# Low parts of weight tiles made by an accumulating DMA instead of DVE subtractions, in a two-layer diffusion block

## The chip, the core and the metric

The kernel runs on one core of one Trainium2 chip. The metric is the device time of one execution in microseconds (us), given as the median of several runs. The engines are called as the profile calls them: PE (matrix multiplications; PEld is its loading of weights), DVE (vector engine), ACT (scalar engine), POOL (GpSimd) and SP (the engine that here only issues loads). The profile also shows the clock that PE was granted, as a share of full speed.

## What is computed

The reference is a block with two layers on 512 latent tokens `x` and 256 context tokens, of width 1024, all in float32. Cut to what matters:

```python
for l in range(2):
    mod = (silu(c) @ w_mod[l] + b_mod[l])            # shifts, scales, gates; the same for c_ctx
    px = (rmsnorm(x, norm1_g[l]) * (1 + sc1) + sh1) @ w_in[l] + b_in[l]
    pc = (rmsnorm(xc, norm1_g[l]) * (1 + scc1) + shc1) @ w_in[l] + b_in[l]
    # columns of px, pc: four mLSTM heads in both directions | spatial gating | convolution
    x = x + g1 * (mix(px) @ w_out[l])
    x = x + g2 * swiglu(rmsnorm(x, norm2_g[l]) * (1 + sc2) + sh2, w_gu[l], w_down[l])
    if l == 0:                                       # the same two lines for the context xc
        ...
return rmsnorm(x, final_g)
```

`w_gu` is 1024 x 5632 and `w_down` 2816 x 1024. Nearly all the work is the multiplication of tokens by these weights, which have to be read from memory: the kernel moves 173 MB.

## The kernel before

**Tiles.** The 768 tokens lie transposed in on-chip memory, features on the 128 partitions. A matmul takes 128 x 128 of a weight tile against 512 latent tokens (`HA`) or 256 context tokens (`HB`). Float32 accuracy comes from splitting both factors into a high part, rounded to the type that PE multiplies in (fp32r), and a low part, the remainder. Each product is then three matmuls, high by high (L453), high by low (L454) and low by high (L455), in `mm` of `tiles`. So only the third needs a weight tile's low part.

**How a weight tile is made.** SP loads it (`loader`, L327) into one of 4 `raw` buffers. ACT rounds it into `hi` (`splitter`, L412); then DVE writes `lo` = raw - hi (`split_lo`, L333), after which the raw buffer is free for another load and the tile may be used. There are 5 pairs of `hi` and `lo`; PE frees one with the last matmul of the tile. The file has 170 such plain tiles: 116 with 1024 columns a partition (512 KB), and 54 narrower ones of 544 to 896.

**Tiles of other kinds.** The weights of the modulation (`w_mod`) are multiplied in float32 as they come, without a split; those of layer 0 come first, in 16 loads of 512 KB into 10 larger buffers called `slot`, and each is used by 8 small matmuls (L595). In the FFN of layer 1, after two plain pairs of columns, 20 "pairs" of columns go through sums and differences of half tiles, as in Strassen's scheme, to save matmuls. Their high parts are cast by ACT (L350), their low parts (L354) and sums (L359) made by DVE, from two loads each (L316), and PE uses them in L1783 to L1785, whose results ACT copies out (L1851). In between stand the plain tiles of `w_down`, called d tiles here: four groups of 8, with 768, 768, 640 and 640 columns, of which three groups stand among the pairs and one at the end.

**The order of the work.** Every engine runs its instructions in the order of the program. That order is made when the program is built, by a planner (`Plan`): each piece of work is a generator that yields costs for an engine (`DVE2`, `ACT`, `POOL`, `PE`, `DMA`, from small formulas in ns), events to wait for and buffers to take, and the planner walks through time and lets the earliest go first. So a cost in these formulas doesn't change how long an instruction takes on the chip, but it does change where it and others stand in the order. For a load the planner adds 2000 ns until its data are there (`DMA_LAT`). The order of the first loads is a string, `EARLY_LOADS`.

**POOL** has little to do before: 42 small instructions for the inverse roots of the norms (L262, tiles `rs`, `srs`, `crs`, `hrs`) and some fills. It issues no DMA. At the start the first tokens are normed with such roots into `HA` and `HB`.

Of the kernel before, what the change touches and what calls it, by code (L numbers as in the profile page):

```python
# [7 lines left out]
F32 = mybir.dt.float32  # L8
F32R = mybir.dt.float32r
AF = mybir.ActivationFunctionType  # L10
ALU = mybir.AluOpType
# [46 lines left out]
class Plan:  # L58
# [12 lines left out]
    def spawn(self, gen, prio=1):  # L71
        t = self.cur.t + LAT if self.cur else 0.0
        self.start(Thread(gen, prio, t))
# [43 lines left out]
    def release(self, name, n=1):  # L117
        t = self.cur.t + LAT
        self.buf[name] += [t] * n
        self.wake(name)  # L120
# [12 lines left out]
    def fire(self, ev, extra=0.0):  # L133
        ev.t = self.cur.t + LAT + extra
        for th in ev.waiting:
            th.t = max(th.t, ev.t)
            th.engine = None
            self.start(th)
        ev.waiting = []
# [27 lines left out]
def W(ev):  # L167
    return ("w", ev)


def A(name, n=1):
    return ("a", name, n)
# [14 lines left out]
def DVE2(n):  # L187
    return ("e", "dve", 65 + 1.04 * n)
# [14 lines left out]
def ACT(n, table=None):  # L203
    return ("e", "act", 95 + 0.833 * n, table)
# [7 lines left out]
    return ("e", "dma", 20 + nbytes / 360.0)  # L212


DMA_LAT = 2000.0
EARLY_LOADS = "xxxxmmwmmww"
AHEAD = (3, 2, 3, 3)
BUFFERS = {"ps": 8, "slot": 10, "raw": 4, "spl": 5, "hp": 0, "u4": 0, "pb": 4, "wi": 3, "cp": 1, "kk": 2, "hc": 2, "C0": 5, "C1": 5}
# [3 lines left out]
def backbone(ctx, tc, xT_d, cT_d, wmod_d, wb_d, wgv_d, wv_d, wout_d, wgu_d, wd_d, sw_d, sb_d, cv_d, rv_d, id_d, mk_d, out_d):  # L222
    nc = tc.nc
    pe, dve, act, pool, sp = nc.tensor, nc.vector, nc.scalar, nc.gpsimd, nc.sync
    S = Plan(BUFFERS)
# [11 lines left out]
    def buf(tag, shape, name, dt=F32):  # L237
        return bufp.tile(shape, dt, tag=tag, name=name, bufs=BUFFERS["spl" if tag in ("hi", "lo") else tag])
# [32 lines left out]
    def ev(*key):  # L271
        if key not in EV:
            EV[key] = Event()
        return EV[key]

    def wsrc(key):
        kind = key[0]
        if kind == "b":
            return wb_d[key[1], key[2]], KD, P
        if kind == "gv":  # L280
            k0, n = GV_SLABS[key[2]]
            return wgv_d[key[1], :, k0 * 272:(k0 + n) * 272], n, 272
        if kind == "v":
            return wv_d[key[1], :, key[2] * 1024:(key[2] + 1) * 1024], 2, 512
        if kind == "o":
            return wout_d[key[1], key[2]], KD, P
        if kind == "gu":
            return wgu_d[key[1], key[2]], KD, P
        if kind == "d":
            j0, n = FFN_GROUPS[key[1]][key[2]]  # L290
            return wd_d[key[1], key[3], :, j0 * P:(j0 + n) * P], n, P
        if kind == "mod":
            return wmod_d[key[1], key[2], key[3]].rearrange("p (a b) -> p a b", a=4), 4, 256
        if kind == "modq":
            _, l, v, q, k = key
            return wmod_d[l, v, 4 * k:4 * k + 4, :, q * 256:(q + 1) * 256].rearrange("k p c -> p k c"), 4, 256
        if kind == "modh":
            _, l, v, half, k = key
            return wmod_d[l, v, 2 * k:2 * k + 2, :, half * 512:(half + 1) * 512].rearrange("k p c -> p k c"), 2, 512
        raise ValueError(kind)  # L300

    def loader():
        for i, key in enumerate(ORDER):
            if key[0] == "x":
                yield DMA(P * T * 8)
                sp.dma_start(out=xT[:, key[1]:key[1] + 2, :], in_=xT_d[:, key[1]:key[1] + 2, :])
                fire(ev("x", key[1]), DMA_LAT)
                continue
            if key[0] == "gp":
                if key[3] == 0:  # L310
# [7 lines left out]
                    RAW[key[:3]] = rs  # L318
                    fire(ev("raw", key[:3]), DMA_LAT)
                continue  # L320
# [6 lines left out]
            sp.dma_start(out=r if key[0][:3] == "mod" else r.rearrange("p a b -> p (a b)"), in_=src)  # L327
            fire(ev("raw", i), DMA_LAT)

    def split_lo(i, hi, lo):  # L330
        r = RAW.pop(i)
        yield DVE2(r.shape[1] * r.shape[2])
        dve.tensor_tensor(lo, r, hi.bitcast(F32), ALU.subtract)  # L333
        release("raw")
        fire(ev("w", i))

# [41 lines left out]
    def split_pair(i, key):  # L378
        u, us = key[3], USET.setdefault(key[:3], {})
        if u == 3:  # L380
            return
        yield A("spl")
        us[u] = take_spl(i)
        if u:
            fire(ev("u", key[:3], u))
            return
        yield A("u4")
        us[3] = SPL[INDEX[key[:3] + (3,)]] = U4.pop(0)
        yield W(ev("raw", key[:3]))
        spawn(pair_sums(key, us), 0)  # L390
# [3 lines left out]
    def splitter():  # L394
        for i, key in enumerate(ORDER):
            if key[0] == "x":
                continue
            if key[0] == "gp":
                yield from split_pair(i, key)
                continue  # L400
            yield W(ev("raw", i))
            if key[0][:3] == "mod":
                SPL[i] = RAW.pop(i)
                fire(ev("w", i))
                continue
            _, a, b = wsrc(key)
            yield A("spl")
            hi = buf("hi", [P, a, b], "hi", F32R)
            lo = buf("lo", [P, a, b], "lo", F32R)
            SPL[i] = (hi, lo)  # L410
            yield ACT(a * b)
            act.copy(hi, RAW[i])  # L412
            spawn(split_lo(i, hi, lo), 0)

    prog = []
# [426 lines left out]
    def layer(l):  # L842
# [13 lines left out]
        def E(*key):  # L856
            return ev(l, *key)
# [47 lines left out]
        def gv_pre():  # L905
# [12 lines left out]
            for half in range(2):  # L918
                yield DMA(64 * 256 * 4)
                sp.dma_start(out=st["bs"][64 * half:64 * half + 64], in_=sb_d[l, half].partition_broadcast(64))  # L920
            fire(E("gvc"), DMA_LAT)

# [37 lines left out]
        def gates(gi):  # L960
# [87 lines left out]
            st["dr"] = dr  # L1048
            fire(E("dr"), DMA_LAT)
            yield A("ps")  # L1050
# [181 lines left out]
        def v_pre():  # L1232
# [5 lines left out]
            for i in range(2):  # L1238
                v_[i] = slot([P, 3, H, P + 1], "v")
                yield POOL(12)  # L1240
                pool.memset(v_[i][:, :, :, P:P + 1], 1.0)
            fire(E("bv"), DMA_LAT)

# [761 lines left out]
    ppos, mpos, nx = [], [], 0  # L2005
    for c in EARLY_LOADS + "m" * len(pkeys) + "w" * len(mkeys):
        n = len(ORDER)
# [17 lines left out]
    with tc.manual_schedule():  # L2025
        S.spawn(start(), 0)
        S.spawn(loader(), 3)
        S.spawn(splitter(), 0)
        S.spawn(main(), 5)
        try:  # L2030
            S.run()
        except AssertionError:
            for k, e in EV.items():
                if e.t is None and e.waiting:
                    print("EV", k, [(t.gen.__name__, t.gen.gi_frame.f_lineno) for t in e.waiting])
            raise
# [64 lines left out]
```

## Time and profile before

| What | Before |
|---|---|
| median of 3 runs | 1569.12 us (1568.55 to 1570.35) |
| profiled execution | 1569.28 us |
| its span, first to last instruction | 1567.5 us |
| mean granted clock of PE | 0.994 |
| data moved | 173.21 MB, mean 111 GB/s |

The rows of the profile that the prediction uses are shown there. A row of a group gives line, engine, operation, tiles out<-in, shapes and count, then busy us and mean ns of one, then the idle time of the engine just before these instructions and what ended it. "PE mm L453 <- ACT HA L1523: 1.2, 1, 1.2" in the list of waits says that PE, at L453, was idle for what ACT's L1523 made: us in all, how often, longest. A row of the timeline starts with the time in the span and the duration, and may end with a wait in brackets.

### The profile page before, as it was taken

What the parts mean: (1) busy time and instruction counts of PE and PEld (TensorE: products, weight loads), DVE (VectorE), ACT (ScalarE), POOL (GpSimd) and SP (SyncE); (2) the same over time, 40 slices, a digit from 0 to 9 for tenths busy, and PEclk for the clock granted to TensorE, in tenths of its full rate; (3) what the DMA queues carried; (4) which work ended last, traced back from release to release, by engine and by line L of the source; (5) the groups of instructions that cost most, each with busy time, mean ns of one, the idle gap of its engine ahead of it and who ended that gap; (6) DMA issues with size and microseconds to landing.
All of it is one profiled execution on the core that took longest, in us unless ns stands there. A gap on an engine that the chain in (4) does not pass through costs nothing.

```text
span 1567.5 us, 25687 instructions
## 1 busy us (share of the span) xinstructions
PE 1525.9 (97%) x10472; PEld 1360.0 (87%) x10472; DVE 966.2 (62%) x1934; ACT 590.3 (38%) x1128; POOL 30.9 (2%) x50
## 2 busy tenths in 40 slices
PE   4999999999999999999999999999999799999997
PEld 3887888888888888888888888878999799999997
DVE  4449877456655555433444345496777886776775
ACT  4332267543322211221122234415664454443443
POOL 0000011000000000000000000000000000000000
PEclk9999999999999999999999999999999899999999
DMA  9434344312243334433343211322331133233331
GB/s 325 150 111 140 106 131 149 141 54 82 81 136 121 110 105 136 134 120 101 130 148 109 93 62 62 102 76 88 115 109 55 55 121 95 96 101 102 105 111 55
DMA packets 69362, 173.21 MB, mean 111 GB/s; under 512 B 7180, under 2 KB 18556, under 8 KB 69244
## 3 DMA queue, kind: packets, MB, share of 16 engines
q1 hardware_dynamic: 66476, 170.16, 33.1%
q8 instruction: 82, 1.34, 0.3%
q10 hardware_dynamic: 2768, 1.42, 0.3%
q14 instruction: 36, 0.29, 0.1%
HBM read 169.34 MB, written 2.21 MB: 109 GB/s over the span
## 4 chain that ended last, share of the span: by engine, by line
PE 94%; DVE 3%; DMA 1%; ACT 1%; issue 1%; SPq 0%; POOLq 0%; POOL 0%; DVEq 0%; ACTq 0%
PE mm L453 23%; PE mm L454 22%; PE mm L455 22%; PE bA L1785 2%; PE bA L1783 2%; PE bA L1784 2%; PE vp L1224 2%; PE vp L1226 1%; PE vp L1225 1%; PE bC L1785 1%; PE bC L1783 1%; PE bC L1784 1%; PE stp L1361 1%; PE num L1445 1%; PE num L1448 1%; PE modps L575 1%
## 5 line engine op out<-in xcount | busy, mean ns | idle before, releaser
L453 PE MATMUL mm<-HA,hi 128*128 128x512 f32 (+1 forms) x928 | 347.0, 374 | 1.7 <-ACT HA L1523 1.2
L454 PE MATMUL mm<-HA,hi 128*128 128x512 f32 (+1 forms) x928 | 337.9, 364 | 1.3 <-DVE HA L790 1.0
L455 PE MATMUL mm<-HA,lo 128*128 128x512 f32 (+1 forms) x928 | 337.4, 364 | 0.0
L412 ACT CAST hi<-raw 128x1024 fp32r<-128x1024 f32 (+5 forms) x170 | 165.9, 979 | 406.4 <-PE mm L454 148.3
L333 DVE TENSOR_TENSOR lo<-raw,hi 128x1024 fp32r<-128x1024 f32 (+5 forms) x170 | 192.5, 1135 | 159.9 <-ACT hi L412 151.9
L453 PEld LDWEIGHTS mm<-HA,hi 128*128 128x128 f32 x928 | 175.1, 189 | 31.4 <-issue 4.7
L455 PEld LDWEIGHTS mm<-HA,lo 128*128 128x128 f32 x928 | 174.5, 188 | 29.9
L454 PEld LDWEIGHTS mm<-HA,hi 128*128 128x128 f32 x928 | 175.0, 189 | 25.8 <-DVE HA L790 1.9
L453 PE MATMUL mm<-HB,hi 128*128 128x256 f32 x592 | 170.1, 287 | 0.0
L823 DVE SCALAR_TENSOR_TENSOR xT<-mm,modc,xT 128x256 f32<-128x256 f32 (+1 forms) x144 | 77.4, 542 | 146.3 <-PE mm L455 145.5
L454 PE MATMUL mm<-HB,hi 128*128 128x256 f32 x592 | 165.0, 279 | 0.8 <-DVE HB L790 0.8
L455 PE MATMUL mm<-HB,lo 128*128 128x256 f32 x592 | 164.8, 278 | 0.0
L453 PE MATMUL mm<-hid,hi 128*128 128x256 f32 (+1 forms) x352 | 119.6, 340 | 0.0
L453 PEld LDWEIGHTS mm<-HB,hi 128*128 128x128 f32 x592 | 111.3, 188 | 8.8 <-issue 5.4
L455 PE MATMUL mm<-hid,lo 128*128 128x256 f32 (+1 forms) x352 | 118.7, 337 | 0.0
L454 PE MATMUL mm<-hid,hi 128*128 128x256 f32 (+1 forms) x352 | 118.4, 336 | 0.0
L454 PEld LDWEIGHTS mm<-HB,hi 128*128 128x128 f32 x592 | 112.2, 190 | 3.8 <-DVE HB L790 1.0
L455 PEld LDWEIGHTS mm<-HB,lo 128*128 128x128 f32 x592 | 111.3, 188 | 0.0
L647 DVE SCALAR_TENSOR_TENSOR macc<-raw,csil,macc 128x512 f32<-128x512 f32 x140 | 101.6, 746 | 0.7
L454 PE MATMUL mm<-ffn,hi 128*128 128x256 f32 x352 | 99.1, 282 | 0.3 <-DVE ffn L1886 0.3
L453 PE MATMUL mm<-ffn,hi 128*128 128x256 f32 x352 | 99.1, 281 | 0.1
L455 PE MATMUL mm<-ffn,lo 128*128 128x256 f32 x352 | 98.4, 280 | 0.0
(302 smaller groups left out, 2993.7 us busy)
## 6 DMA issues: line engine op xcount, KB each, us to landing
raw<-in_wmod SPq DMA_DIRECT2D x96, 512.0 KB, 3.7
raw<-in_wgu SPq DMA_DIRECT2D x88, 512.0 KB, 3.5
raw<-in_wb SPq DMA_DIRECT2D x36, 512.0 KB, 3.5
pbt<-dr SPq DMA_DIRECT2D x40, 256.0 KB, 3.6
raw<-in_wout SPq DMA_DIRECT2D x16, 512.0 KB, 3.5
raw<-in_wd SPq DMA_DIRECT2D x16, 448.0 KB, 3.9
raw<-in_wd SPq DMA_DIRECT2D x16, 384.0 KB, 3.3
raw<-in_wd SPq DMA_DIRECT2D x16, 320.0 KB, 3.0
```

The costliest lines, as they stand in the source:

```text
L333: dve.tensor_tensor(lo, r, hi.bitcast(F32), ALU.subtract)
L412: act.copy(hi, RAW[i])
L453: pe.matmul(o, lhsT=hi[:, k, :], rhs=hh, start=(j == 0), stop=False)
L454: pe.matmul(o, lhsT=hi[:, k, :], rhs=hl, start=False, stop=False)
L455: pe.matmul(o, lhsT=lo[:, k, :], rhs=hh, start=False, stop=(j == nk - 1))
L575: pe.matmul(p[32 * c:32 * c + 32, 0:256], lhsT=csil[:, k, :], rhs=s[:, c, :], start=(k == 0), stop=(k == KD - 1), skip_group_check=True)
L647: dve.scalar_tensor_tensor(a[:, g, :], s[:, i, :], c, a[:, g, :], ALU.mult, ALU.add)
L823: dve.scalar_tensor_tensor(x, p[:, 0:n], MODC[l][:, v, d, g:g + 1], x, ALU.mult, ALU.add)
L1224: pe.matmul(out, lhsT=hh, rhs=hi[:, kk, :], start=(k == 0), stop=False)
L1783: pe.matmul(o, lhsT=hi[:, k], rhs=rh[:, k], start=start and k == 0, stop=False, skip_group_check=True)
L1784: pe.matmul(o, lhsT=hi[:, k], rhs=rl[:, k], start=False, stop=False, skip_group_check=True)
L1785: pe.matmul(o, lhsT=lo[:, k], rhs=rh[:, k], start=False, stop=k == 3, skip_group_check=True)
```

## The change

`lo` is no longer a subtraction on DVE. ACT writes minus `hi` into `lo` right behind the cast (a second ACT instruction of the same size, on the same tile), and POOL then issues a DMA that adds the raw tile to it in place, element by element, so that `lo` = -hi + raw. The DMA's landing, not an instruction's end, now frees the raw buffer and makes the tile ready. The planner counts 1.0 us of POOL for the issue and 4.0 us more until it has landed. POOL's buffer for DMA descriptors is doubled. This holds for the 170 plain tiles; the pairs of layer 1's FFN keep DVE for their low parts.

```diff
+def POOLQ():
+    return ("e", "pool", 1000.0)
+
 DMA_LAT = 2000.0
+ADD_LAT = 4000.0
...
     def split_lo(i, hi, lo):
         r = RAW.pop(i)
-        yield DVE2(r.shape[1] * r.shape[2])
-        dve.tensor_tensor(lo, r, hi.bitcast(F32), ALU.subtract)
+        yield POOLQ()
+        pool.dma_start(out=lo, in_=r, accum_op=ALU.add)
+        S.cur.t += ADD_LAT
         release("raw")
         fire(ev("w", i))
...
             yield ACT(a * b)
             act.copy(hi, RAW[i])
+            yield ACT(a * b)
+            act.mul(lo, hi.bitcast(F32), -1.0)
             spawn(split_lo(i, hi, lo), 0)
...
-    nc = bacc.Bacc("TRN2", target_bir_lowering=False, num_devices=1, dynamic_dma_scratch_size=1024)
+    nc = bacc.Bacc("TRN2", target_bir_lowering=False, num_devices=1, dynamic_dma_scratch_size=2048)
```

Since the planner's costs change, so does the order. In the changed file lines stand 5 to 8 further down: the matmuls L453 to L455 are L461 to L463, the modulation's L595 is L603, the cast L412 is L418, the new ACT instruction is L420 and the new DMA L338.

At the start of PE's order before, these rows follow the first two modulation loads (`x8` is one load's matmuls; `mm` the first weight tile, on context tokens):

```order
4 L595 MATMUL modps<-raw,csil 32x128 x16
5 L766 MATMUL rstdb<-ident,rs 128x128 x2
6 L612 MATMUL modT<-sel_80,mq 128x4
7 L766 MATMUL rstdb<-ident,rs 128x128 x4
8 L595 MATMUL modps<-raw,csil 32x128 x8
9 L453 MATMUL mm<-HB,hi 128x256
10 L454 MATMUL mm<-HB,hi 128x256
11 L455 MATMUL mm<-HB,lo 128x256
12 L595 MATMUL modps<-raw,csil 32x128 x16
```

And these stand there in PE's order after:

```order
4 L603 MATMUL modps<-raw,csil 32x128 x8
5 L774 MATMUL rstdb<-ident,rs 128x128 x2
6 L603 MATMUL modps<-raw,csil 32x128 x8
7 L620 MATMUL modT<-sel_80,mq 128x4
8 L774 MATMUL rstdb<-ident,rs 128x128 x4
9 L603 MATMUL modps<-raw,csil 32x128 x16
10 L620 MATMUL modT<-sel_80,mq 128x4
11 L603 MATMUL modps<-raw,csil 32x128 x16
12 L620 MATMUL modT<-sel_80,mq 128x4
13 L603 MATMUL modps<-raw,csil 32x128 x8
14 L461 MATMUL mm<-HB,hi 128x256
```

With the first two, five modulation loads stood ahead of the first weight matmul; now nine do.

On ACT, in the paired FFN columns of layer 1, the order before around a d tile of `w_down` (L412) was this (L350 are casts of the pairs' weights, L1851 copies of results that wait for PE, `d` and `x` on `bA`):

```order
741 L350 CAST hi<-raw 128x1024
742 L350 CAST HA<-raw 128x4x128
743 L412 CAST hi<-raw 128x768
744 L1851 COPY d<-bA 128x256
745 L350 CAST hi<-raw 128x1024
746 L1851 COPY x<-bA 128x256
747 L350 CAST hi<-raw 128x1024
748 L412 CAST hi<-raw 128x768
749 L1875 ACTIVATE x<-x 128x512
```

After, at the same place:

```order
927 L356 CAST hi<-raw 128x1024
928 L356 CAST HA<-raw 128x4x128
929 L418 CAST hi<-raw 128x768
930 L1859 COPY d<-bA 128x256
931 L420 ACTIVATE lo<-hi 128x768
932 L356 CAST hi<-raw 128x1024
933 L1859 COPY x<-bA 128x256
934 L356 CAST hi<-raw 128x1024
935 L418 CAST hi<-raw 128x768
936 L420 ACTIVATE lo<-hi 128x768
937 L1883 ACTIVATE x<-x 128x512
```

The new instruction stands right behind the second cast, but for the first tile behind a copy that was next after the cast. PE's own order in this stage is the same before and after.

POOL's order at the start, before, held only the small instructions:

```order
7 L262 TENSOR_TENSOR rs<-ms,ex_78 128x2
8 L262 TENSOR_TENSOR rs<-ms,ex_78 128x4
9 L262 TENSOR_TENSOR srs<-smv,ex_78 128x6
10 L1241 MEMSET v 128x12 x2
11 L262 TENSOR_TENSOR crs<-cmv,ex_78 128x1 x5
```

After, the adds stand among them:

```order
7 L267 TENSOR_TENSOR rs<-ms,ex_78 128x2
8 L338 DMA lo<-raw 128x1024
9 L267 TENSOR_TENSOR rs<-ms,ex_78 128x4
10 L338 DMA lo<-raw 128x1024 x3
11 L338 DMA lo<-raw 128x816 x2
12 L338 DMA lo<-raw 128x544
13 L338 DMA lo<-raw 128x1024 x3
14 L267 TENSOR_TENSOR srs<-smv,ex_78 128x6
```

The second norm's root (row 9, for the latent tokens) now stands behind the first tile's add.

## The prediction

> **What bounds the kernel now.** I read the page's busy line and its chain first, then what PE waited for, then the stages, by windows.
>
> ```profile
> PE 1525.9 (97%) x10472; PEld 1360.0 (87%) x10472; DVE 966.2 (62%) x1934; ACT 590.3 (38%) x1128; POOL 30.9 (2%) x50
> PE 94%; DVE 3%; DMA 1%; ACT 1%; issue 1%; SPq 0%; POOLq 0%; POOL 0%; DVEq 0%; ACTq 0%
> ```
>
> The first line is the busy time of each engine, the second the share of each in the chain that ended last. PE works 97% of the span and makes 94% of the chain; DVE, from which the change takes work, has 62% and is in the chain for 3%. So the 192 us of subtractions are no sum that can be won. Won or lost is only time in which PE stands still, 41.6 us of the 1567.5. The waits of PE, longest first, and the two groups of instructions that make a weight tile's two parts (count, busy us, mean ns):
>
> ```profile
> PE modps L595 <- DMA raw<-in_wmod: 17.2, 2, 16.9
> PE bC L1785 <- DVE lo L354: 4.1, 1, 4.1
> PE bC L1783 <- ACT hi L350: 3.8, 1, 3.8
> PE bA L1785 <- DVE lo L354: 1.7, 1, 1.7
> PE mm L453 <- ACT HA L1523: 1.2, 1, 1.2
> ...
> L412 ACT CAST hi<-raw 128x1024 fp32r<-128x1024 f32 (+5 forms) x170 | 165.9, 979 | 406.4 <-PE mm L454 148.3
> L333 DVE TENSOR_TENSOR lo<-raw,hi 128x1024 fp32r<-128x1024 f32 (+5 forms) x170 | 192.5, 1135 | 159.9 <-ACT hi L412 151.9
> ```
>
> 17.2 us is the first weight load at the start, which nothing here touches. 9.6 us (4.1 + 3.8 + 1.7) belong to the start of the paired FFN columns, whose low parts stay on DVE (L354). No wait names L333, the instruction that goes: its tiles were always ready. The casts of L412 waited 148.3 us for PE to free a buffer (L454), so tiles are made as early as the buffers allow. Three stages, by windows (us, then busy time of each engine, granted clock, DMA share, GB/s):
>
> ```profile
> core 0: us, PE busy (x) PEld busy (x) DVE busy (x) ACT busy (x) POOL busy (x), PEclk, DMA share, GB/s
> 27.70:33.90 6.20, 3.78 (x48) 2.78 (x43) 5.80 (x10) 3.27 (x6) 0.00 (x0) 0.93 1.09 362
> 33.90:49.90 16.00, 16.00 (x200) 11.89 (x199) 9.26 (x22) 5.78 (x12) 0.00 (x0) 0.92 0.82 288
> ...
> 1200.00:1220.00 20.00, 20.00 (x176) 19.98 (x176) 19.64 (x41) 10.65 (x22) 0.70 (x1) 1.00 0.02 6
> 1220.00:1240.00 20.00, 10.29 (x67) 9.31 (x66) 18.32 (x23) 10.72 (x14) 0.00 (x0) 0.74 0.17 53
> ...
> 1280.00:1360.00 80.00, 80.00 (x690) 80.00 (x690) 58.18 (x92) 34.93 (x51) 0.00 (x0) 1.00 0.32 103
> ```
>
> At 27.7 to 33.9 PE still has holes (3.78 of 6.20) and the DMA engines are full (1.09); from 33.9 PE has none. At 1200 to 1240 DVE is the full engine (38 of 40 us). At 1280 to 1360 PE is full, and there the weight tiles come just in time, as shown below.
>
> **The change, part by part.** *The price of an add, X*, from POOL's issue to the landing, is in no row, since POOL issues no DMA before. Its nearest rows are loads of the same sizes by SP (KB, median us to landing) and POOL's own small instruction (0.70 us):
>
> ```profile
> raw<-in_wgu SPq DMA_DIRECT2D x88, 512.0 KB, 3.5
> raw<-in_wd SPq DMA_DIRECT2D x16, 384.0 KB, 3.3
> raw<-in_wd SPq DMA_DIRECT2D x16, 320.0 KB, 3.0
> raw<-in_wd SPq DMA_DIRECT2D x8, 512.0 KB, 4.1
> L262 POOL TENSOR_TENSOR hrs<-ss,ex 128x2 f32<-128x2 f32 x20 | 14.0, 701 | 129.8 <-DVE ss L1475 107.4 <-DVE dn L1456 16.4 <-DVE gs L777 6.0
> ```
>
> Low end: a plain load, 3.3 us for 384 KB and 3.0 for 320. High end: the bytes are read twice, raw and lo, so two loads, and POOL's 0.7: 7.3 and 6.7. From 320 to 512 KB of w_down the loads grow by 1.1 us, 5.7 ns a KB; so I take one load, one more pass of moving and POOL's 0.7: 3.3 + 2.2 + 0.7 = 6.2 us, 3.0 + 1.8 + 0.7 = 5.5, and 3.5 + 2.9 + 0.7 = 7.1 for 512 KB of other weights. It is nearer to the high end, because the add has a second operand for certain. The Trainium skill, page DMA: Bandwidth & Descriptors, section Anatomy of one DMA, gives a POOL-issued transfer 2.0 us and its bytes over 436 GB/s, which is an estimate of 2.9 us for 384 KB, with no word on a second operand; by that the waits for lo below would be nothing and the sum 3.8 us. No run here shows a POOL-issued DMA yet.
>
> *Paired FFN columns, layer 1.* PE's order is the same there before and after. Casts, the copies between them, and the first matmul that uses each lo:
>
> ```profile
> 1280.53 0.83 ACT L412 CAST hi<-raw 128x768 fp32r<-128x768 f32 x1
> 1287.51 0.28 PE L455 MATMUL mm<-ffn,lo 128*128 128x256 f32 x1
> ...
> 1304.11 0.84 ACT L412 CAST hi<-raw 128x768 fp32r<-128x768 f32 x1 [1.13 <-PE bC L1784]
> 1312.58 0.28 PE L455 MATMUL mm<-ffn,lo 128*128 128x256 f32 x1
> 1312.54 0.83 ACT L412 CAST hi<-raw 128x768 fp32r<-128x768 f32 x1
> 1316.08 0.37 ACT L1851 COPY d<-bA 128x256 f32<-128x256 f32 x1 [2.70 <-PE bA L1785]
> 1323.74 0.28 PE L455 MATMUL mm<-ffn,lo 128*128 128x256 f32 x1
> ...
> 1469.16 0.72 ACT L412 CAST hi<-raw 128x640 fp32r<-128x640 f32 x1
> 1472.34 0.37 ACT L1851 COPY d<-bA 128x256 f32<-128x256 f32 x1 [2.46 <-PE bA L1785]
> 1479.65 0.28 PE L455 MATMUL mm<-ffn,lo 128*128 128x256 f32 x1
> ```
>
> Now ACT writes minus hi (priced as the cast), then POOL's add must land. For the first tile of a group: 1280.53 + 0.83 + 0.83 = 1282.2, used at 1287.5, which leaves 5.3 us for X. For every other tile 1304.11 + 1.68 to 1312.58: 6.8 us. Between them stand tiles whose minus hi is behind a copy that waits for PE: 1316.08 + 0.37 + 0.83 to 1323.74 leaves 6.5; with 640 columns 1472.71 + 0.73 to 1479.65 leaves 6.2. Of these 24 tiles 16 have 768 columns, in two groups. With X = 6.2 only the two first ones wait, 0.9 us each: +1.8. With 5.5 the 640s don't. A raw buffer is also held until the add has landed, on which SP's next load waits; at X = 6.2 that load still lands before its cast. ACT has room for 0.8 us a tile (34.93 of 80).
>
> *The start.* The planner counts 1.0 + 4.0 us for an add, so it puts the first weight matmul behind nine modulation loads instead of five (the order shows it). Those loads are issued at 1.55 us each (18.62 / 12), and a load takes 7.7 us in this crowd:
>
> ```profile
> 17.10 18.62 SPq L327 DMA_DIRECT2D raw<-in_wmod  x12
> 27.74 0.38 PE L453 MATMUL mm<-HB,hi 128*128 128x256 f32 x1
> 27.70:33.90 6.20, 2.48 (x9) 1.75 (x9) 0.00 (x0) 0.00 (x0) 0.93 1.09 362
> 10.51 7.72 DMA raw<-in_wmod
> 26.20 1.05 ACT L412 CAST hi<-raw 128x1024 fp32r<-128x1024 f32 x1
> ```
>
> The first matmul moves from 27.74 by 4 x 1.55 to 33.9 at least. The 2.48 us of mm work that stood in those holes (third row, by tile) must be done after 33.9, where PE had no hole: +2.5. The first add goes through DMA engines that are full, so loads up to the ninth land later by one to two slots, 1.6 to 3.1; I take 2.0. The adds of the next two tiles delay later loads by 3 to 6 us, which costs nothing: the last is issued at 35.7, lands some 7.7 us later and is used at 49, six us of cover. The second tile's minus hi ends at 26.20 + 2.1 = 28.3, its add at 36 if it takes a crowded load's 7.7, about when PE wants it: 0 to 3, taken 0.5. The clock rows lose 0.07 x 6.2 + 0.08 x 16 = 1.7 us of PE, a stretch at half clock after the thin start; thinner now, it may last up to twice that: taken 0.5. Sum of the start +5.5, bounds +2.5 (the moved work alone) and +10.3.
>
> *Relief of DVE.*
>
> ```profile
> 1196.20 1.22 DVE L333 TENSOR_TENSOR lo<-raw,hi 128x1024 fp32r<-128x1024 f32 x1
> ```
>
> This one stands in the stretch where DVE is full up to the 9.6 us of PE waits at 1224 to 1235; without it that row of work moves up by 1.2 us: -1.2, bounds -3 and 0. In all other stages DVE has room and PE no wait, so relief buys nothing; X is covered there, since PE needs some 17 us for a tile in layer 0 and holds several.
>
> **Sum**: 1569.28 (the profiled execution; its span is 1567.5, the median of the runs 1569.12) + 5.5 + 1.8 - 1.2 = 1575.4; I say 1575.5.
>
> **Rivals.** *The start is hidden* (0.23). The adds slip between loads and the later order of PE fills its holes as well as the earlier: 2.5 - 1.2 = +1.3 us, 1570.5, no change. For it: PE is busy 97% of the time in whatever order. Against: a full PE after 33.9 leaves no hole for work that was put off.
>
> *Slow adds* (0.17). X at its high end, or past it. It decides from 6.2 us on, the smallest cover of all but the two first tiles. At 7.3 and 6.7: 2 x 2.0, 7 x 0.5 and 7 x 0.8 for the other 768s, 8 x 0.5 for the 640s, 17 us, with 10.3 at the start and -1.2: 1595. Each further us of X adds 24.
>
> *Faster* (0.07). On the other side: the relief of DVE decides. If the start costs nothing because the adds land in half the time taken, PE gets back 1.2 us at 1196, up to 1.2 of the wait for HA (L1523) behind DVE at the end of layer 1's heads, and one stretch less at half clock after 1224 (0.26 x 20 = 5.2 us are lost there; a third is 1.7): -4.1, 1565. It decides once the start costs under 1 us. Against it: the moved first matmul costs 2.5 by itself.
>
> *POOL is late* (0.03). If POOL can't make its transfers while DVE holds a shared port, every add starts up to one DVE instruction (1.22 us) later, DVE being busy 58 of 80 us: X = 7.4 and 6.7, the waits of the slow adds, with the start at 5.5: 1591. The Trainium skill, SBUF — State Buffer, section Who interferes with whom, says so of copies and tensor-scalar forms on DVE, and that two-input forms leave descriptor making alone. No run here shows either.
>
> **How the numbers follow.** The forecast (1573 to 1583) has 0.50. A measurement tells 0.2%, 3.1 us, from no change. Slower by more: 0.50 + 0.17 + 0.03 = 0.70; same 0.23; faster 0.07. The range leaves out the faster case and the tail of the slow adds, X over 7.7 (1595 + 24 x 0.45 = 1606): 1568 to 1606.
>
> **What would show it.** L333 gone from DVE, some 750 us on ACT, PE busy as before; the first mm at 34 to 37 us; PE waiting for a DMA that writes lo at two tiles of the paired stage and nowhere else; 1224 to 1235 a little shorter. I am wrong if PE waits on lo in the 768s in every block (adds over 6.5 us), if the first mm comes without later loss, or if PE waits for POOL's small instructions behind an add.

## The result, and the profile after

| What | Before | After |
|---|---|---|
| median | 1569.61 us (4 runs, 1568.55 to 1570.35) | 1606.13 us (4 runs, 1603.17 to 1610.88) |
| ratio to before | | 1.0235 (1.0221 to 1.0249) |
| profiled execution, its span | 1569.28, 1567.5 us | 1603.34, 1601.6 us |

The change costs 36.5 us, six times what was forecast. The page of after, busy line and shares of the chain:

```profile
PE 1536.6 (96%) x10472; PEld 1363.6 (85%) x10472; DVE 792.8 (49%) x1764; ACT 743.2 (46%) x1298; POOL 180.7 (11%) x220
PE 75%; DMA 13%; issue 4%; DVE 4%; ACT 2%; POOL 0%; SPq 0%; POOLq 0%; DVEq 0%; ACTq 0%
```

DVE lost 173 us of busy time and ACT gained 153; that is a little less than the 192 us of subtractions and the 168 us of minus hi, because neighbouring instructions overlap in this count. The end is still set by PE, but its share of the chain fell from 94% to 75%, and DMA now has 13%. Outside PE's busy time there are 65.0 us of the span (1601.6 - 1536.6), against 41.6 before: 23.4 more. And the same 10472 matmuls are busy 10.7 us longer, for which the lower mean clock can account (0.986 against 0.994, 0.008 of 1537 us is 12). Together 34.1, the difference of the spans.

What PE waited for in after, longest first:

```profile
PE modps L603 <- ACT sq L721: 16.4, 1, 16.4
PE mm L461 <- ACT HA L1531: 7.6, 1, 7.6
PE modps L603 <- DMA raw<-in_wmod: 6.8, 5, 4.4
PE mm L463 <- DMA lo<-raw: 5.7, 5, 2.0
```

The first row is the wait for the first load (before: 17.2, named after another event). New or longer are HA (1.2 before), the modulation's weights at the start, and lo.

Where the time comes from can be read by progress. All kernels run 10472 matmuls in nearly the same sequence; I number them by their start and compare the time at which the same number starts. Worked out so from the traces, in us, before as time and the others as difference to it:

| matmul number, stage that ends there | before | after | order only (e1) | ACT part (e6) | allowance 5.4 (f1) | mended (g1) | mended, 5 buffers (g6) | heads only (g5) |
|---|---|---|---|---|---|---|---|---|
| 700, the start | 101.8 | +6.6 | -1.9 | +0.5 | +7.6 | -2.2 | -2.6 | -2.2 |
| 2200, heads and w_out, layer 0 | 328.9 | +11.5 | +3.8 | +2.2 | +10.2 | +0.2 | +1.9 | +0.3 |
| 3700, FFN of layer 0, first part | 578.9 | +11.0 | +5.5 | +2.1 | +10.7 | +1.1 | +2.0 | -0.3 |
| 5500, FFN of layer 0, rest | 884.6 | +22.7 | +10.2 | +2.2 | +20.2 | +15.9 | +7.8 | +0.2 |
| 7000, heads of layer 1 | 1136.0 | +22.7 | +16.1 | +2.0 | +20.4 | +16.9 | +8.0 | +0.4 |
| 7300, their end and w_out | 1172.8 | +30.0 | +23.1 | +7.2 | +20.5 | +17.4 | +8.0 | +0.4 |
| 10471, the last | 1561.3 | +33.6 | +23.4 | +10.8 | +25.4 | +18.7 | +8.2 | +1.4 |

After loses in five places: 6.6 at the start, 4.9 in layer 0's heads, 11.7 in the second part of layer 0's FFN, 7.3 at the end of layer 1's heads, 3.6 in the paired columns and the end.

The groups that make a tile's parts, and the adds from issue to landing (KB, median us):

```profile
L418 ACT CAST hi<-raw 128x1024 fp32r<-128x1024 f32 (+5 forms) x170 | 166.3, 978 | 332.7 <-DMA raw<-in_wgu 110.6
L420 ACT ACTIVATE lo<-hi 128x1024 fp32r<-128x1024 f32 (+5 forms) x170 | 167.8, 987 | 2.5
L338 POOL DMA_DIRECT2D lo<-raw x170 | 148.0, 871 | 1241.7 <-ACT lo L420 944.2
...
lo<-raw POOLq DMA_DIRECT2D x116, 512.0 KB, 5.4
...
lo<-raw POOLq DMA_DIRECT2D x16, 384.0 KB, 4.8
```

Minus hi costs ACT what the cast costs, as priced. The adds are faster than the 7.1 and 6.2 us that the forecast took. So X isn't what went wrong. The casts now wait for loads (L418), where before they waited most for PE to free a buffer: tiles are late. The chain of after in layer 0's FFN shows why (start, us, what):

```profile
589.89 3.46 DMA raw<-in_wd
...
600.45 3.64 DMA raw<-in_wd
604.16 1.07 ACT hi L418
605.25 1.07 ACT lo L420
606.32 0.34 issue
606.67 4.55 DMA lo<-raw
611.27 3.44 DMA raw<-in_wgu
614.79 1.05 ACT hi L418
615.87 1.06 ACT lo L420
616.92 0.16 ACT modsb L550
617.13 0.48 PE modT L556
```

This is a ring. A load starts when the add of the tile before it has landed and freed its raw buffer; it takes 3.5 us; cast, minus hi and issue take 2.5; the add takes 4.5. One turn is 10.6 to 10.8 us (589.89 to 600.45 to 611.27). There are four raw buffers, but only one seems to go round for tiles here. Between two tiles SP issues one load of layer 1's modulation weights (at 590.31 and 600.87); that these hold the other three is inferred from this, not shown. SP's loads stood 386 us for subtractions in before and 872 us for adds in after:

```profile
SPq L327 <- DVE lo L333: 385.8, 94, 22.8
```

```profile
SPq L332 <- DMA lo<-raw: 872.1, 144, 21.7
```

PE needs a tile much more often, as the windows of before show, here for the matmuls of weight tiles alone (us, then busy time and count of PE, PEld, DVE and ACT):

```profile
480.00:560.00 80.00, 78.99 (x455) 68.84 (x455) 6.48 (x11) 3.49 (x7) 1.00 0.36 121
```

A w_gu tile is 8 x 3 x 2 = 48 matmuls, so 455 are 9.5 tiles in 80 us, one every 8.4 us. Before, a turn had 1.2 us of DVE in place of 1.1 + 4.9, and the ring kept ahead. In after each turn of such a ring loses some 2 us until PE waits. Modulation pays too: in the last rows its copy (`modsb`) stands on ACT behind a cast that waits for such a load, and PE's `modT` waits for the copy.

Some waits cost more than their length. Windows of after around four of them (us; busy and count of PE, PEld, DVE, ACT, POOL; granted clock, DMA share, GB/s), three at the start, one behind a wait of 1.63 us for lo at 789, two around one of 2.05 us at 887, and one behind the wait for HA:

```profile
33.90:36.00 2.10, 1.67 (x18) 1.10 (x18) 0.31 (x1) 0.27 (x1) 0.00 (x0) 0.50 1.03 220
36.00:41.00 5.00, 0.60 (x12) 0.64 (x16) 3.74 (x8) 1.63 (x3) 0.00 (x0) 0.50 1.06 297
41.00:49.90 8.90, 8.90 (x105) 6.27 (x97) 0.92 (x4) 1.15 (x3) 0.00 (x0) 0.85 1.10 355
...
792.00:800.00 8.00, 8.00 (x53) 6.60 (x53) 1.61 (x4) 2.38 (x3) 0.00 (x0) 1.00 0.78 232
...
886.00:890.00 4.00, 1.95 (x17) 1.76 (x17) 0.00 (x0) 1.21 (x2) 0.00 (x0) 1.00 0.88 167
890.00:900.00 10.00, 10.00 (x45) 8.48 (x44) 2.29 (x5) 2.76 (x5) 0.86 (x1) 0.83 0.67 171
...
1183.00:1195.00 12.00, 12.00 (x87) 11.80 (x88) 5.93 (x17) 3.16 (x9) 0.00 (x0) 0.83 0.32 96
```

After the waits of 2.05 and 7.6 us the clock is 0.83 for 10 and 12 us: 1.7 and 2.0 us more. After the one of 1.63 us it is 1.00. At the start the clock of 0.50 mostly met a PE that stood idle. Where PE was busy it lost 0.5 x 1.67 + 0.5 x 0.60 + 0.15 x 8.90 = 2.5 us, against 1.3 in before.

### The profile page after: what moved, and what is told of

Same layout as the page of the kernel before. It is cut to its first block, busy times and chain, and to the rows that moved or that the text cites. A ratio compares the mean times of both kernels' runs of the same rounds, so it can differ in the third digit from the quotient of the medians.

```text
span 1601.6 us, 26138 instructions
## 1 busy us (share of the span) xinstructions
PE 1536.6 (96%) x10472; PEld 1363.6 (85%) x10472; DVE 792.8 (49%) x1764; ACT 743.2 (46%) x1298; POOL 180.7 (11%) x220
## 3 DMA queue, kind: packets, MB, share of 16 engines
q0 software_dynamic: 24480, 81.93, 28.5%
## 4 chain that ended last, share of the span: by engine, by line
PE 75%; DMA 13%; issue 4%; DVE 4%; ACT 2%; POOL 0%; SPq 0%; POOLq 0%; DVEq 0%; ACTq 0%
PE mm L461 18%; PE mm L463 18%; PE mm L462 18%; DMA lo<-raw 6%; DMA raw<-in_wd 3%; PE bA L1793 2%; PE bA L1792 2%; PE bA L1791 2%; DMA raw<-in_wmod 2%; DMA pbt<-dr 1%; PE num L1453 1%; PE num L1456 1%; PE vp L1232 1%; PE bC L1793 1%; PE vp L1233 1%
## 5 line engine op out<-in xcount | busy, mean ns | idle before, releaser
L461 PE MATMUL mm<-HA,hi 128*128 128x512 f32 (+1 forms) x928 | 348.0, 375 | 7.6 <-ACT HA L1531 7.6
L463 PE MATMUL mm<-HA,lo 128*128 128x512 f32 (+1 forms) x928 | 337.7, 364 | 0.0
L418 ACT CAST hi<-raw 128x1024 fp32r<-128x1024 f32 (+5 forms) x170 | 166.3, 978 | 332.7 <-DMA raw<-in_wgu 110.6
L338 POOL DMA_DIRECT2D lo<-raw x170 | 148.0, 871 | 1241.7 <-ACT lo L420 944.2
L461 PEld LDWEIGHTS mm<-HA,hi 128*128 128x128 f32 x928 | 175.9, 189 | 37.6 <-ACT HA L1531 7.8
L463 PEld LDWEIGHTS mm<-HA,lo 128*128 128x128 f32 x928 | 175.6, 189 | 30.1
L461 PE MATMUL mm<-HB,hi 128*128 128x256 f32 x592 | 169.6, 287 | 0.0
L420 ACT ACTIVATE lo<-hi 128x1024 fp32r<-128x1024 f32 (+5 forms) x170 | 167.8, 987 | 2.5
L463 PE MATMUL mm<-HB,lo 128*128 128x256 f32 x592 | 165.5, 280 | 2.5 <-DMA lo<-raw 2.4
L1699 DVE TENSOR_TENSOR s<-s,mm 128x256 f32<-128x256 f32 (+1 forms) x48 | 26.0, 542 | 192.4 <-PE mm L463 161.1
L463 PE MATMUL mm<-hid,lo 128*128 128x256 f32 (+1 forms) x352 | 119.3, 339 | 1.6 <-DMA lo<-raw 1.6
L461 PE MATMUL mm<-hid,hi 128*128 128x256 f32 (+1 forms) x352 | 120.0, 341 | 0.0
L461 PEld LDWEIGHTS mm<-HB,hi 128*128 128x128 f32 x592 | 111.8, 189 | 7.5 <-issue 4.6
L463 PEld LDWEIGHTS mm<-HB,lo 128*128 128x128 f32 x592 | 111.8, 189 | 3.1 <-DMA lo<-raw 3.1
L463 PE MATMUL mm<-ffn,lo 128*128 128x256 f32 x352 | 98.7, 280 | 1.8 <-DMA lo<-raw 1.6
```

The source lines that it names most:

```text
L338: pool.dma_start(out=lo, in_=r, accum_op=ALU.add)
L420: act.mul(lo, hi.bitcast(F32), -1.0)
L461: pe.matmul(o, lhsT=hi[:, k, :], rhs=hh, start=(j == 0), stop=False)
L463: pe.matmul(o, lhsT=lo[:, k, :], rhs=hh, start=False, stop=(j == nk - 1))
L1699: dve.tensor_tensor(s, s, pu[:, 0:n], ALU.mult)
```

## The experiments

The theories at the outset were these. **Order**: the planner's new order makes the loss. **Chain**: the add holds a tile and its raw buffer longer, so loads come late. **ACT**: the 168 us of minus hi stand in front of what PE waits for. First four kernels: three with the order of PE as in after or as in before, row by row, and one with a fifth raw buffer.

**e1_order**, after's plan with the subtraction:

```diff
-            act.mul(lo, hi.bitcast(F32), -1.0)
-        pool.dma_start(out=lo, in_=r, accum_op=ALU.add)
+        dve.tensor_tensor(lo, r, hi.bitcast(F32), ALU.subtract)
```

> The planner's order of after, word for word on PE, but the low part is again the subtraction on DVE: no minus-high on ACT, no add. Order theory (the later order of the start and of the heads makes most of the loss): about 1569.3 + 6.6 at the start + 5 in layer 0's heads + 7 at the end of layer 1's heads = 1588, and PE then still waits some 7 us for HA near 1175. Chain theory (a tile takes longer to make, since its raw buffer is held until the add has landed): only the start remains, 1569.3 + 2 to 6 = 1571 to 1576, and layer 0's FFN is as fast as before. ACT theory (168 us more work on ACT, which stands in front of HA and of the modulation): as the chain theory.

1594.5 us, 1.0161 (1.0145 to 1.0176): more than half of the loss without a single add. The start is 1.9 us *ahead* of before. The wait for HA is there (6.7). This kernel has a flaw as a measure of the order: its plan doesn't know of the 192 us of subtractions that DVE does, which probably puts its heads behind their plan (12.9 us between matmuls 5500 and 7300, HA included).

**e2_order_mul**, the same with minus hi on ACT left in, overwritten by the subtraction.

> As the order-only kernel, but ACT also writes minus high into lo, which DVE's subtraction then overwrites: ACT's share of the change without the DMA. ACT theory: slower than the order-only kernel by 7 us or more, with the wait for HA at the end of layer 1's heads at about 7.6 us as in after. Chain theory: within 3 us of the order-only kernel. Order theory: within 3 us of it, both near 1588.

1599.8 us, 1.0186 (1.0170 to 1.0202): 5.3 more than e1, which is between the theories; 3.4 of it is at the start (+1.5 by the count of the table). The wait for HA is 7.6, as in after.

**e3_add_old_order**, before's plan, with minus hi and add written in, and no cost for either in the planner:

```diff
             act.copy(hi, RAW[i])
+            act.mul(lo, hi.bitcast(F32), -1.0)
...
         yield DVE2(r.shape[1] * r.shape[2])
-        dve.tensor_tensor(lo, r, hi.bitcast(F32), ALU.subtract)
+        pool.dma_start(out=lo, in_=r, accum_op=ALU.add)
```

> The planner's order of before (PE as before), but with minus-high on ACT and the add from POOL. Order theory: most of the loss is gone, 1569.3 + 3 to 10. Chain theory: the loss in layer 0's FFN is there or larger, since the order leaves no allowance for the add: PE waits for lo there in sum 5 us or more, 1569.3 + 15 to 40 = 1584 to 1610. ACT theory: 7 to 9 us at the end of layer 1's heads, and little in the FFN.

1744.4 us, 1.1117 (1.1093 to 1.1142). All expectations were far too low. PE hardly waits for lo; it waits for the modulation of layer 1, whose weights share the raw buffers with the tiles:

```profile
PE modT L549 <- ACT modsb L543: 45.7, 10, 10.9
PE modps L658 <- DVE macc L648: 38.5, 11, 9.6
...
PE mm L456 <- DMA lo<-raw: 2.0, 3, 1.2
```

I read this so: an order that promises tiles too early makes in-order engines stand behind the late ones. Then the order of after isn't the culprit as such: it is needed, and its allowance is too short.

**e4_raw5**, after with five raw buffers.

> The changed kernel with five raw buffers instead of four (the room comes from POOL's descriptor buffer, back at its size in before). Chain theory: the loads of layer 0's FFN no longer wait for the add of the tile just before, the waits for lo there (6 us) and for the modulation's weights at 612 (5 us with the half clock) go, 1606 - 11 = 1595 or less. Order and ACT theories: no more than 3 us better, about 1603 to 1606.

1608.7 us, 1.0245 (1.0219 to 1.0271): no gain. The waits for lo went, but PE waits 7.3 us at 655 and 2.4 at 619 for `modsb`. With the plan's 4 us the chain theory failed this test.

Next, before's own kernel with one part of the plan at a time.

**e5_late**: `S.cur.t += 4000.0` behind the subtraction. **e6_act**: minus hi on ACT, counted, and overwritten. **e7_jolt**: the subtraction counted for 100 elements more. **e8_late3**: e5's line for the first three tiles alone.

> The kernel before with its subtraction on DVE, and one line more in the planner: a tile counts as ready, and its raw buffer as free, 4.0 us after the subtraction. No instruction is added; only the order changes. Lateness theory (the 4 us in the plan spoil the order of the heads): 1569.6 + 12 or more, with PE idle for some 7 us for HA at the end of layer 1's heads. ACT-charge theory (the planner counts 1 us more of ACT for each tile, and puts the heads' last steps later): 1569.6 + 0 to 5, no long wait for HA. Any-shift theory (the order of before is a lucky one, and whatever moves it costs about as much): 1569.6 + 8 to 20.

> The kernel before with its subtraction on DVE, and minus-high written by ACT into lo first (overwritten by the subtraction), with its 1 us of ACT counted by the planner: the ACT part alone, planned as in after. ACT-charge theory: 1569.6 + 12 to 20, PE idle some 7 us for HA at the end of layer 1's heads. Lateness theory: 1569.6 + 2 to 6, the 5 us that the same ACT work cost on top of the order-only kernel. Any-shift theory: 1569.6 + 8 to 20.

> The kernel before, with nothing changed but one cost in the planner: the subtraction counts as if a row were 100 elements longer, some 0.1 us more of DVE a tile. A control for how much the time moves with the order alone. Any-shift theory: 1569.6 + 8 or more. Lateness and ACT-charge theories: within 3 us of 1569.6.

> The kernel before, with the planner's 4 us of lateness for the first three tiles alone: nearly the start's order of after (eight loads of modulation weights before the first weight matmul), the rest as before. Prediction on record (later first matmul costs 2.5 us): 1572. From the order-only kernel, which was 1.9 us ahead of before at 100 us: 1567 to 1568.

e5 1572.9 us, 1.0028 (1.0019 to 1.0038). e6 1582.5 us, 1.0084 (1.0066 to 1.0102). e7 1569.8 us, 1.0001 (0.9991 to 1.0011). e8 1569.3 us, 0.9995 (0.9986 to 1.0005). The any-shift theory falls with e7. Lateness alone costs 3 us. ACT's part alone costs about 13 in the medians, and e6's longest new wait of PE is

```profile
PE mm L455 <- ACT HA L1525: 4.1, 1, 4.1
```

e8 has eight modulation loads ahead of the first weight matmul and isn't slower: the start's later order costs nothing.

**f1_lat54**: `ADD_LAT = 5400.0`. **f3_act_late**: e6 and e5 together. **f4_copy**: the add without `accum_op`, so that lo holds the raw tile. **f5_first3**: after's order, the first three tiles subtracted on DVE.

> The changed kernel with the planner's allowance for an add raised from 4.0 to 5.4 us, the median that the trace shows. Allowance theory (the plan promises tiles too early, and work behind them on the in-order engines stands still): the start and layer 0's FFN lose less, 1606 - 5 to 15 = 1591 to 1601. Hold theory (the raw buffers are held too long whatever the plan says, so loads come late): 1603 to 1610, waits for lo in layer 0's FFN as they are.

> The kernel before with both things that the plan of after also has, but no add: minus-high on ACT (overwritten by the subtraction, planned), and the planner's 4.0 us of lateness. If the parts add up: 1569.6 + 12.8 + 3.2 = 1585.6. What is left to after's 1606.1 is then the adds themselves and the plan without DVE's work. If the two together upset the order more than each (order theory): 1594 or more, as the order-only kernel.

> The changed kernel with a plain DMA of the same bytes from POOL in place of the add, so that lo holds the raw tile and the output is wrong. If adding costs (two operands read): median of issue to landing for 512 KB down from 5.4 to about 4 us, and the time nearer to 1595. If a POOL-issued DMA costs the same with and without the add: 5.0 to 5.5 us and 1600 to 1610.

> The changed kernel, same order on PE, but the low parts of the first three tiles are subtracted on DVE instead of added by DMA. If the adds among the crowded loads make the start's 6.6 us: 1606 - 5 to 7 = 1600. If it is ACT's minus-high or the order there: 1604 to 1608.

f1 1594.4 us, 1.0164 (1.0146 to 1.0183): 1.4 us more in the plan for each tile give back 11.7. Mostly this is the end of layer 1's heads: no wait of PE in f1 names the HA of L1531 any more, and that stage is at +0.1 where after lost 7.3. The time lies in the range of the allowance theory, but not for its reason: the start (+7.6) and the second part of layer 0's FFN (9.5) lose about as much as in after. The waits for lo stay, as the hold theory said:

```profile
PE mm L463 <- DMA lo<-raw: 9.2, 9, 2.8
```

f3 1591.7 us, 1.0146 (1.0131 to 1.0162): 22 to 23 where the parts gave 16, so the plan's changes don't add up. f5 1599.6 us, 1.0198 (1.0183 to 1.0213): 6.5 less than after, and its start is at +1.6, so the first adds among the crowded loads make 5.0 of after's 6.6 there. f4, a single run, 1587.0 us, 16 below after's profiled execution and below what either theory expected; its order of PE is that of after, row by row. The queue of POOL in after and then in f4, and f4's times:

```profile
q0 software_dynamic: 24480, 81.93, 28.5%
```

```profile
q0 software_dynamic: 24480, 81.93, 14.9%
...
lo<-raw POOLq DMA_DIRECT2D x116, 512.0 KB, 3.3
```

The add takes the DMA engines 1.9 times as long as a copy of the same bytes, and 5.4 us in place of 3.3.

The last five ask what is left when the known losses are mended.

**g1_mend**: allowance 5.4; the first three tiles and the d tiles of layer 1 go back to DVE (`by_add(i)` chooses add or subtraction in `split_lo`, and minus hi in `splitter`, each with its cost). **g4_relief**: the add only for the 12 tiles ahead of the paired columns. **g2_hold**: e1 with an add of the raw tile into a buffer that nobody reads, and a small copy on POOL ahead of it. **g5_heads**: g1 with layer 0's FFN on DVE. **g6_mend_raw5**: g1 with five raw buffers.

> The adds kept only where the other runs do not charge them: the first three tiles and the 32 tiles of layer 1's paired columns go back to DVE (without minus-high on ACT, and counted so in the plan), the other tiles keep the add, planned with 5.4 us. If the parts add up: 1594.4 - 6.5 at the start - 5 in the paired columns = 1583. If the order of the heads, which the plan makes anew, is the larger thing: anywhere from 1575 to 1595, with the start and the paired columns as in before.

> The relief of DVE by itself: only the 12 tiles just ahead of the paired columns of layer 1 (eight of w_out, four of w_gu) are made by the add, planned with 5.4 us; all else as before. The prediction on record gives -1.2 us (0 to 3): 1568.4. If DVE's chain at 1196 to 1235 never held those subtractions: 1569.6, with the waits of 1.7, 3.8 and 4.1 us there unchanged; with ACT's minus-high in front of HA, up to 1574.

> The order-only kernel (subtraction on DVE, order of after) with an add from POOL of the same raw tile into a buffer that nobody reads, issued once lo is ready: the raw buffer is held and the DMA engines are loaded as in after, but the tile itself is ready some 5 us earlier. POOL also makes a small copy for each. Against the order-only kernel's 1594.5. Hold theory (loads come late because raw buffers come free late): most of the adds' loss is there, 1601 to 1608, with waits for the weights in layer 0's FFN and at the start. Readiness theory (only the later landing of lo costs): 1594 to 1597, no wait in the FFN of layer 0 but the one near 607.

> As the mended kernel, with layer 0's FFN back on DVE too (without minus-high on ACT, counted so in the plan): the add is left to w_in from its fourth tile, w_out and four tiles of w_gu. FFN theory (what the mended kernel still loses, 16.9 us, is the chain load, cast, minus-high, add of one tile after the other in layer 0's FFN): 1586.2 - 15 = 1569 to 1573. If the adds cost wherever they stand: 1578 or more.

> As the mended kernel (adds in layer 0's FFN too, planned with 5.4 us) with five raw buffers (room from POOL's descriptor buffer). Hold theory (in that FFN the modulation's weights of layer 1 occupy the raw buffers but one, which goes round in 11 us where PE takes a tile each 8.3): the waits for lo of 10 us there go, 1586.2 - 10 to 15 = 1571 to 1576. If the landing alone is too late, however many buffers: 1583 to 1588. If modulation falls behind instead, as with five buffers and the allowance of 4 us: 1580 or more, with waits named after the modulation.

g1 1586.2 us, 1.0107 (1.0093 to 1.0121): the start is 2.2 us ahead of before, the heads lose 3.9 in all, and 14.8 of what is left stand between matmuls 3700 and 5500. Its second wait:

```profile
PE mm L472 <- DMA lo<-raw: 10.3, 5, 3.5
```

g5 1571.4 us, 1.0019 (1.0010 to 1.0029): without layer 0's FFN the loss is 2 us. g6 1577.3 us, 1.0057 (1.0042 to 1.0072): with the fifth buffer PE has no wait for lo left, 9 of the 17 us are back, and the longest new wait is

```profile
PE modT L565 <- ACT modsb L559: 3.0, 1, 3.0
```

Beside g1 it has the same adds and one buffer more that goes round (its plan is made anew with it, and POOL's descriptor buffer is that of before), which supports the ring as the cause in that FFN. g2 1652.2 us, 1.0519 (1.0503 to 1.0535), says little: POOL waited 304 us for its one shared target, and small POOL work behind it came late. g4 1571.1 us, 1.0007 (0.9999 to 1.0016): no gain. Two of its three waits at the paired columns are those of before (4.1 and 3.8), and the third is 2.1 us in place of 1.7:

```profile
PE bA L1801 <- DVE lo L367: 2.1, 1, 2.1
```

## Why the prediction was wrong

**The sign was right, the size wrong**: +6 forecast, +36.5 measured.

*"In all other stages DVE has room and PE no wait, so relief buys nothing; X is covered there, since PE needs some 17 us for a tile in layer 0 and holds several"* is the step that failed. It puts every stage but the start and the paired columns at nothing, and 23.9 of after's 33.6 us came there (4.9, 11.7 and 7.3), for two reasons.

*The ring in layer 0's FFN.* A tile is in use for 17 us, but two are in use at once, so PE wants a new one every 8.4. The prediction compared X with the time to the first use in the paired stage only. Elsewhere it should have summed the ring, load 3.5, cast 1.1, minus hi 1.1, issue 0.3, add 4.5, 10.5 us, and set it against 8.4. After loses 11.7 us in the stretch where PE waits on that ring; g5, which takes the adds out of that FFN, loses 0.5. But the ring isn't all of it. With the order of PE of after, row by row, e1 and e2 lose 4.7 and 5.8 us there without any add, with a wait of 2.9 us for the modulation, and f4 loses 3.1 with its shorter copies (e2 and f4 counted as in the table). So the add by itself makes some 6 to 9 of the 11.7.

*No term for the heads.* The change puts an ACT instruction in front of everything on ACT, and the prediction said only that ACT has room in the paired stage. At the end of layer 1's heads PE has nothing left but HA, and HA stands behind ACT:

```profile
1175.11 0.23 PE hT L1493 x2
...
1176.28 0.94 ACT hi L418
...
1177.53 0.96 ACT lo L420
...
1178.79 1.28 ACT L1319
1180.09 2.19 ACT og L1319 x4
1182.28 0.61 ACT HA L1531 x2
```

Before, such a chain was there, but PE had weight matmuls to fill it and waited 1.2 us. In after none is left behind the last `hT`, and the wait is 7.6 us; with the clock behind it this stage loses 7.3 in the table. Minus hi itself is 0.96 of it (e1, the same order without it, waits 6.7); the order is the rest. f1, with the same instructions and 1.4 us more in the plan, has no such wait. Which step of the planner leaves matmuls over in one plan and not in the other wasn't found.

*The start, +5.5*: 6.6 came, from other terms. "The moved work alone" (+2.5) was nothing: e8 and e1 moved it and were 0.9 and 1.9 us ahead. Minus hi on ACT, which has no term there, cost 3.4 (e2 against e1), and the first adds among full DMA engines 5.0 (after against f5): -1.9 + 3.4 + 5.0 is 6.5. The first weight matmul came at 41.4 us and not at 34 to 37, behind a wait of 4.4 us for one load of modulation weights. The lower clock, taken at 0.5, cost 1.2 (2.5 - 1.3). The prediction's own clock terms, here and at 1220 to 1240, count time in which PE stood idle.

*Paired columns, +1.8*: 3.6 came from there to the end. PE's waits for lo were 0.9 and 0.7 us, at two tiles, as forecast, but that is luck: they were the last tile of the first group and the second of the next, not the first of each. X was smaller than taken and the waits came all the same, because a median isn't what a tile sees. From the chain of after:

```profile
1370.76 0.85 ACT hi L418
1371.63 0.85 ACT lo L420
1372.49 0.34 issue
1372.83 7.40 DMA lo<-raw
1380.27 0.39 PE mm L463
```

This add of 384 KB took 7.4 us beside other loads, where the median is 4.8 (over all adds 3.6 to 9.7). The prediction's slack was right: 6.8 us wasn't enough for 7.4. Another 0.7 us were two waits for a copy (`d`, L1859), ahead of which ACT now writes a minus hi; the rest wasn't traced to a cause.

*Relief of DVE, -1.2*: 0 in the time of g4, but not because the reading was wrong. The subtraction at 1196 stood in the chain of before:

```profile
1196.20 1.22 DVE lo L333
1197.42 0.39 DVE nt L813
```

Counted as in the table, g4 is at -0.5 at matmul 7500, beside it, and at -1.3 at 7700, so the row of work did move up, by 0.8; after moves by the same (from +29.3 to +28.5). At 7750, behind the waits at the start of the paired columns, g4 is at -0.1 and after at +29.7. In g4 one wait there is 0.4 us longer, and the lower clock lasts longer, as the last column but two shows, in before and then in g4:

```profile
1234.00:1240.00 6.00, 5.33 (x33) 5.33 (x34) 4.36 (x5) 1.09 (x2) 0.00 (x0) 0.67 0.54 175
```

```profile
1234.00:1240.00 6.00, 6.00 (x30) 6.00 (x30) 3.39 (x3) 0.37 (x1) 0.00 (x0) 0.52 0.53 175
```

Why the clock took back what the relief gave wasn't tested.

*Rivals.* "Slow adds" named the right kind of price, at the wrong place and with the wrong deciding point (X over 6.2 in the paired stage, where the median was 4.8). That the end of its tail, 1606, is the time measured is luck. "POOL is late" didn't happen: each issue on POOL took 0.86 us in the median and none over 1.03. Of the 170 issues 59 had no DVE instruction beside them and 95 only such with two inputs, and both groups have that median. The Trainium skill, SBUF — State Buffer, section Who interferes with whom, has it, as an inference, that two-input forms on DVE leave descriptor making alone, and the row agrees for the work that DVE still does.

What stays open: the 4.9 us of layer 0's heads, of which e5 has 3.6 (-0.7 to 2.9) by lateness in the plan alone; the part of the order in the 11.7 us of layer 0's FFN; and why ACT's part and lateness together cost more than their sum (f3).

## What to carry to other kernels

When an operation that makes tiles gets slower, sum the whole ring that a buffer goes through (load, convert, add, and back to the load) and set it against the time between two tiles, not against how long one tile is in use. In a kernel whose order is planned, give the planner the cost as measured: an allowance 1.4 us too small cost 12 us here, and without any the loss was 175. Taking work from an engine that is hardly in the chain that ends last buys next to nothing, here with 192 us of it.

## What the hardware showed

- A DMA from POOL that adds into its target took 5.4 us for 512 KB on chip, a plain copy 3.3, with 28.5% and 14.9% of the DMA engines' time; the issue on POOL was 0.86 and 0.53 us. The Trainium skill, DMA: Bandwidth & Descriptors, section Anatomy of one DMA, gives 2.0 us and the bytes over 436 GB/s, an estimate of 3.2 us for 512 KB: the copy agrees, the add doesn't.
- PE's clock was 0.83 over the 10 us that follow a wait of 2.05 us, which cost 1.7 us more; over the 8 us behind a wait of 1.63 us it was 1.00.
